# Tile addresses at multiples of 512 bytes, and a final norm split between two engines, in a two-layer trunk

## The chip, the cores and the metric

The kernel runs on one core of one Trainium2 chip. The metric is the time of one execution on the device, in microseconds. The engines are named as in the profile: PE (TensorE's matmuls), PEld (its weight loads), DVE (VectorE), ACT (ScalarE), POOL (GpSimd) and SP (SyncE, which here only issues transfers).

## The reference

A float32 trunk of two layers on 512 tokens of 1024 channels. Layer 0 mixes with a gated linear recurrence (LRU), layer 1 with a sparse attention of three branches; each is followed by a gated FFN with a short convolution, and the whole ends with one more norm:

```python
for layer in range(DEPTH):
    h = h + mixer(rmsnorm(h, mixer_norm_g), ...)          # LRU in layer 0, attention in layer 1
    h = h + conv_ffn(rmsnorm(h, ffn_norm_g[layer]), ...)  # (gelu(conv(a)) * b) @ w_out, 3072 wide
return rmsnorm(h, final_norm_g)
```

```python
def rmsnorm(x, g):
    y = x * lax.rsqrt(jnp.mean(x * x, axis=-1, keepdims=True) + EPS)
    return y * g
```

## The kernel before

Channels lie on the 128 partitions, tokens along the columns, so the activation `x` is 8 tiles of 128 x 512 float32. Every large product is made of three matmuls of 512 columns (`mm3`, lines 211 to 218): weights and activations are each split into a high and a low part in a reduced float32 format, and high x high, high x low and low x high are summed in PSUM. The activation is the moving operand; the weights, 128 x 128 at a time, are the stationary one. ScalarE makes the high part of a weights tile of 128 x 1024, DVE the low part (`_split`, line 178), some tiles ahead of their use. A weights tile serves 8 such slices, 24 matmuls. `wtile` (line 151) puts two of three weights tiles (`whi`, `wlo`) into the pool `wp`, each third one (`whix`, `wlox`) into the pool `wx`; in the FFN's output two tiles of the first kind, 48 matmuls, and one of the second, 24, follow each other.

Order of the work: LRU input (to 130.76 us of the profiled execution), LRU output (to 188.20), FFN input (to 452.10), FFN output (to 585.44), the attention's projections, its scheduled part (676.10 to 875.55, whose order on all engines is written out by hand with a step for each operation), its output (to 898.12), and the second FFN. The last output tile of the second FFN (`m` = 7) is done in two halves of 256 tokens, so that the final norm of the first half (`final`, line 369) runs under the matmuls of the second. `final` sums the squares by a matmul with a column of ones, takes the power on GpSimd, spreads the result over the partitions with a matmul by the identity (`ident`, in `cst`), and then DVE multiplies 8 tiles in place, each one sent off by a transfer of 128 KB, in turn from SP's and ScalarE's queue.

Where the tiles lie: a pool takes its tiles in the order of their first use, each size rounded up to 32 bytes per partition, and the pools lie one behind the other. In the program before, the constants' pool `cp` starts at byte 16,512 of a partition, which leaves 128 when it is divided by 512. The remainders modulo 512 are:

| tiles | remainder before |
|---|---|
| `cst` | 128 |
| `xh`, `xl` (moving, all input products) | 320 |
| `whi`, `wlo` (stationary) | 320 |
| `whix`, `wlox` (stationary) | 0 |
| `fh`, `fl` (moving, FFN output) | 0 |
| `hh`, `hl`, `ch`, `cl`, `ghi`, `glo` (LRU) | 160 |
| `K2h`, `K2l`, `V2`, `P` (attention) | 0 |
| `qa`, `qb` | 256 |
| `ph` | 64 |
| `oh`, `ol` | 128, from the second half on 0 |

Slices of a tile begin at multiples of 512 bytes in all the large products, so a remainder holds for the whole tile.

Of the kernel before, what the change touches and what calls it, by code (L numbers as in the profile page):

```python
# [10 lines left out]
F32 = mybir.dt.float32  # L11
F32R = mybir.dt.float32r
AF = mybir.ActivationFunctionType
# [4 lines left out]
NT = 512  # L18
KD = 8
NB = 10  # L20
NF = 24
DMA = 3
SSQ = (1, 1, 1, 1)
# [47 lines left out]
P_LRUG, P_NSAG, P_FFNG, P_FING = 0, 8, 16, 32  # L71
# [3 lines left out]
P_END = 380  # L75

C_ID, C_D, C_DC, C_SC, C_ROW, C_ONE, C_SL = 0, 128, 640, 768, 776, 777, 778
C_END = 794
# [22 lines left out]
class Trunk:  # L101
# [166 lines left out]
    def norm_finish(self, newps):  # L268
        T, V = self.T, self.V
        ps = newps()  # L270
        for t in range(4):
            T.matmul(ps[:, t:t + 1], self.ssum[:, 128 * t:128 * t + 128], self.cst[:, C_ONE:C_ONE + 1],
                     start=True, stop=True)
        v = self.np_.tile([128, 4], F32, name="nv", bufs=1)
        V.tensor_scalar(v, ps[:, :4], 1.0 / 1024.0, 1e-6, op0=ALU.mult, op1=ALU.add)
        self.rtok = self.np_.tile([128, 4], F32, name="rtok", bufs=1)
        self.G.tensor_tensor(self.rtok, v, self.mhalf, op=ALU.pow)
# [9 lines left out]


    def start(self):
# [6 lines left out]
        self.mhalf = self.cp.tile([128, 4], F32, name="mhalf")  # L296
        self.V.memset(self.mhalf, -0.5)
        warm = self.cp.tile([128, 4], F32, name="warm")
        self.S.activation(warm, self.mhalf, AF.Copy)
# [12 lines left out]
        nc.sync.dma_start(self.prm[:, P_CW:], a["prm"][:, P_CW:])  # L312
# [10 lines left out]
    def run(self):  # L323
# [33 lines left out]
        if self.next_split or seq[-1][:3] != "ffn":  # L357
            for _ in self.final(slice(0, NT), self.ring(0, 1)):
                pass
# [9 lines left out]
    def final(self, ts, newps, sq=None):  # L369
# [10 lines left out]
        v = self.np_.tile([128, 4], F32, name="fv")  # L380
        V.tensor_scalar(v[:, :n], ps[:, :n], 1.0 / 1024.0, 1e-6, op0=ALU.mult, op1=ALU.add)
        rt = self.np_.tile([128, 4], F32, name="frt")
# [222 lines left out]
    def softplus(self, hp):  # L605
# [18 lines left out]
        sp = hp.tile([128, 2, NB], F32, name="sp")  # L624
# [5 lines left out]
    def ffn(self, l):  # L630
        S, V, prm = self.S, self.V, self.prm
        col = lambda c: prm[:, c:c + 1]
        with ExitStack() as s:
# [36 lines left out]
            if not self.next_split:  # L670

                m = KD - 1
                ws = [self.w() for c in range(3)]
                fin = iter(())
                for hf in range(2):
# [9 lines left out]
                    fin = self.final(ts, newacc, sq[:, :256])  # L685
# [14 lines left out]
    def nsa(self):  # L700
        S, V, G, T, prm, cst = self.S, self.V, self.G, self.T, self.prm, self.cst
        tc, a = self.tc, self.a
        with ExitStack() as s:
# [9 lines left out]
            gtok = kp.tile([128, 4, 48], F32, name="gtok")  # L713
# [188 lines left out]
            junk = self.np_.tile([128, 4], F32, name="nv", bufs=1)  # L902
# [22 lines left out]
            def compressed(g, s0, d, newps=None):  # L925
# [39 lines left out]
                def norm():  # L965
                    sm = st["sm"] = ap_.tile([128, 4, 4], F32, name="smc", bufs=1)
# [41 lines left out]
            def scores(g, i, brs, steps):  # L1008
# [280 lines left out]
```

## Time and profile before

| | |
|---|---|
| median of 3 runs | 1311.29 us (1311.05 to 1311.66) |
| profiled execution | 1311.32 us |
| its span, first to last instruction | 1309.5 us |
| mean granted clock of TensorE | 0.996 |
| busy: PE, PEld, DVE, ACT, POOL | 1295.0, 1062.5, 787.2, 612.8, 242.2 us |

Matmuls are pipelined: one shows some 390 ns of its own, but the next starts long before it ends. So the distance from start to start is what a stretch of matmuls costs, and it is read from the starts in the timeline or as a stage's length by its count. Starts are shown to 0.01 us.

### The profile page before, as it was taken

Reading aid. Unit: us, or ns where it says so; the run is one execution under the profiler, and the core shown is the slowest. Engines: PE = TensorE matmul, PEld = TensorE weight load, DVE = VectorE, ACT = ScalarE, POOL = GpSimd, SP = SyncE. Lnnn points to the kernel's source line nnn. Section 1 sums busy time; section 2 is a strip of 40 time slices with the busy share of each in tenths; the row PEclk is TensorE's granted clock in tenths of the full one; section 3 lists DMA queues with packets and bytes.
Section 4 is the critical chain, followed back from the end, with each engine's and each line's share of the span. In section 5 each row is a group of like instructions: output and inputs, shape, how many; then the busy total and the mean of one; then the engine's idle time right before and its main releaser. Section 6 shows DMA issues by size and latency. Waiting matters only on the chain.

```text
span 1309.5 us, 16269 instructions
## 1 busy us (share of the span) xinstructions
PE 1295.0 (99%) x6158; PEld 1062.5 (81%) x6158; DVE 787.2 (60%) x1270; ACT 612.8 (47%) x983; POOL 242.2 (18%) x254
## 2 busy tenths in 40 slices
PE   9999999999999999999999999999999999999996
PEld 7888888888888888888787778888888888888886
DVE  7899875555555533327557978875655555542222
ACT  6788743333333322222458878865433333332220
POOL 0222440000000001115017667633000000000110
PEclk9999999999999999999999999999999999999998
DMA  7232232232232222223311010113222232222221
GB/s 243 89 100 85 90 97 97 97 97 97 97 97 97 96 98 97 90 101 121 121 66 33 33 33 33 34 33 129 97 97 97 97 97 97 97 97 96 89 73 65
DMA packets 36222, 117.71 MB, mean 90 GB/s; under 512 B 4144, under 2 KB 7728, under 8 KB 36144
## 3 DMA queue, kind: packets, MB, share of 16 engines
q1 hardware_dynamic: 34848, 115.61, 26.5%
q8 instruction: 48, 0.79, 0.3%
q10 hardware_dynamic: 1296, 1.07, 0.2%
q14 instruction: 30, 0.25, 0.1%
HBM read 114.57 MB, written 2.10 MB: 89 GB/s over the span
## 4 chain that ended last, share of the span: by engine, by line
PE 94%; DVE 2%; ACT 1%; issue 1%; POOL 1%; DMA 0%; SPq 0%; POOLq 0%; DVEq 0%; ACTq 0%
PE bank L213 28%; PE bank L214 28%; PE bank L215 27%; PE bank L1081 2%; PE bank L1101 1%; PE bank L1097 1%; PE bank L873 1%; PE bank L1027 1%; PE bank L1028 1%; PE bank L832 1%; PE bank L831 1%; PE bank L833 1%; DVE P L1040 0%; PE bank L1100 0%; ACT P L228 0%
## 5 line engine op out<-in xcount | busy, mean ns | idle before, releaser
L213 PE MATMUL bank<-xh,whi 128*128 128x512 f32 x760 | 297.8, 392 | 0.5 <-DVE qn L754 0.2
L215 PE MATMUL bank<-xh,wlo 128*128 128x512 f32 x760 | 296.2, 390 | 0.5 <-DVE wlo L185 0.5
L214 PE MATMUL bank<-xl,whi 128*128 128x512 f32 x760 | 296.2, 390 | 0.3 <-DVE xl L256 0.3
L184 ACT ACTIVATE whi<-wraw 128x1024 fp32r<-128x1024 f32 x143 | 151.3, 1058 | 303.8 <-PE bank L214 251.1
L185 DVE TENSOR_TENSOR wlo<-wraw,whi 128x1024 fp32r<-128x1024 f32 x133 | 163.5, 1230 | 127.4 <-ACT whi L184 117.0
L266 POOL TENSOR_TENSOR ssum<-ssum,sq 128x512 f32<-128x512 f32 x27 | 44.8, 1658 | 766.3 <-issue 581.1
L213 PEld LDWEIGHTS bank<-xh,whi 128*128 128x128 f32 x760 | 142.8, 188 | 32.5 <-DVE nm L1040 0.8
L215 PEld LDWEIGHTS bank<-xh,wlo 128*128 128x128 f32 x760 | 142.6, 188 | 31.0 <-DVE wlo L185 1.0
L214 PEld LDWEIGHTS bank<-xl,whi 128*128 128x128 f32 x760 | 142.8, 188 | 29.6 <-DVE xl L256 0.8
L184 ACT ACTIVATE whix<-wrawx 128x1024 fp32r<-128x1024 f32 x57 | 60.4, 1060 | 131.0 <-PE bank L214 129.6
L214 PE MATMUL bank<-xl,whix 128*128 128x512 f32 x296 | 116.5, 394 | 0.0
L213 PE MATMUL bank<-xh,whix 128*128 128x512 f32 x296 | 116.1, 392 | 0.0
L215 PE MATMUL bank<-xh,wlox 128*128 128x512 f32 x296 | 115.1, 389 | 0.0
L213 PE MATMUL bank<-fh,whi 128*128 128x512 f32 (+1 forms) x272 | 104.0, 382 | 0.0
L214 PE MATMUL bank<-fl,whi 128*128 128x512 f32 (+1 forms) x272 | 103.9, 382 | 0.0
L215 PE MATMUL bank<-fh,wlo 128*128 128x512 f32 (+1 forms) x272 | 103.9, 382 | 0.0
L1057 POOL TENSOR_SCALAR P<-P,c,gtok 128x512 f32<-128x512 f32 (+3 forms) x128 | 79.4, 634 | 99.9 <-DVE c L1053 85.2
L185 DVE TENSOR_TENSOR wlox<-wrawx,whix 128x1024 fp32r<-128x1024 f32 x57 | 70.8, 1242 | 40.9 <-ACT whix L184 40.8
L648 DVE TENSOR_TENSOR ar<-bank,rbc 128x512 f32<-128x512 f32 x48 | 33.2, 691 | 99.6 <-PE bank L215 99.6
L658 DVE TENSOR_TENSOR b<-bank,rbc 128x512 f32<-128x512 f32 x48 | 33.2, 691 | 86.2 <-PE bank L215 86.2
L228 ACT ACTIVATE P<-P,nm 128x512 f32<-128x512 f32 (+3 forms) x128 | 70.9, 556 | 16.9 <-DVE nm L1040 13.8
L228 ACT ACTIVATE t<-t 128x512 f32<-128x512 f32 x48 | 30.4, 632 | 98.0 <-DVE t L654 98.0
(219 smaller groups left out, 2311.5 us busy)
## 6 DMA issues: line engine op xcount, KB each, us to landing
wraw<-in_ffn_in_dram SPq DMA_DIRECT2D x65, 512.0 KB, 3.3
wraw<-in_ffn_out_dram SPq DMA_DIRECT2D x32, 512.0 KB, 3.3
wrawx<-in_ffn_in_dram SPq DMA_DIRECT2D x31, 512.0 KB, 3.3
wrawx<-in_ffn_out_dram SPq DMA_DIRECT2D x16, 512.0 KB, 3.2
wraw<-in_nsa_in_dram SPq DMA_DIRECT2D x16, 512.0 KB, 3.3
wraw<-in_lru_in_dram SPq DMA_DIRECT2D x12, 512.0 KB, 3.7
w<-in_cmp_w_dram SPq DMA_DIRECT2D x8, 512.0 KB, 4.5
wraw<-in_nsa_out_dram SPq DMA_DIRECT2D x8, 512.0 KB, 3.3
```

The lines of the kernel that those rows point to most:

```text
L184: self.S.activation(hi[:, c], raw[:, c], AF.Copy)
L185: (eng or (self.G if self.manual and WLO else self.V)).tensor_sub(lo[:, c], raw[:, c], hi[:, c].bitcast(F32))
L213: ins = mm(ps, wh, xh, start=first, stop=False)
L214: mm(ps, wh, xl, start=False, stop=False)
L215: end = mm(ps, wl, xh, start=False, stop=last)
L228: ins = self.S.activation(out, in_, func, **k)
L266: self.sq_eng.tensor_add(self.ssum, self.ssum, sq)
L648: V.tensor_mul(ar, pa, self.rbc)
L658: V.tensor_mul(b, pb, self.rbc)
L831: T.matmul(pv[t], xh[:, ts], hi[:, sl], start=(k == 0), stop=False)
L1057: G.tensor_scalar(Ps[g, i, br][r], Ps[g, i, br][r], st["c"][:, br, r:r + 1], gtok[:, i, gc:gc + 1], op0=ALU.mult, op1=ALU.mult)
L1081: T.transpose(st["t", kt][:, 128 * r:128 * r + 128], Ps[u][r][:, 128 * kt:128 * kt + 128], self.ident)
```

## The change

Small tiles that only DVE, ScalarE or GpSimd use (and `gtok`) move from the pools of the stages into `cp`, ahead of `cst` or between `cst` and `prm`; `prm` grows by 4 columns and `sp` from 20 to 112, so that the tiles that follow begin elsewhere. `mx` and `smc` of the attention become one tile. In the final norm the sums of `ssum` for both token blocks come before those of `sq`; ScalarE copies the spread norm to SBUF; GpSimd makes the products of `x` tiles 4, 5 and 6 from that copy, and since it multiplies two operands only, ScalarE scales these three tiles by the norm's gain beforehand; DVE makes the other five. The products go to new tiles of two, and a transfer takes two of them (256 KB). The diff, cut to its core:

```diff
+FG = (4, 5, 6)
 def start(self):
-        self.prm = self.cp.tile([128, P_END], F32, name="prm")
-        self.cst = self.cp.tile([128, C_END], F32, name="cst")
+        one = lambda name, shape: self.cp.tile([128] + shape, F32, name=name)
+        few = lambda name, shape, n: [one(f"{name}{j}", shape) for j in range(n)]
+        self.few = {"sm": few("sm", [2, 4], 3), "nm": few("nm", [2, 4], 2), "c": few("c", [2, 4], 3),
+                    "mx": few("mx", [16], 1)}
+        fv, self.mhalf = one("fv", [4]), one("mhalf", [4])
+        self.cst = one("cst", [C_END])
+        self.gtok = one("gtok", [4, 48])
+        self.nv, self.rtok = one("nv", [4]), one("rtok", [4])
+        self.few["fv"], self.few["frt"] = [self.nv, fv], few("frt", [4], 2)
+        self.prm = one("prm", [P_END + 4])
 def softplus(self, hp):
-        sp = hp.tile([128, 2, NB], F32, name="sp")
+        sp = hp.tile([128, 112], F32, name="sp")[:, :2 * NB].rearrange("p (a n) -> p a n", a=2)
 def final(self, ts, newps, newout, sq=None):
-        for t in range(n):
-            for j, p in enumerate(parts):
+        for j, p in enumerate(parts):
+            for t in range(n):
                 T.matmul(ps[:, t:t + 1], p[:, 128 * t:128 * t + 128], self.cst[:, C_ONE:C_ONE + 1],
-                         start=(j == 0), stop=(j == len(parts) - 1))
+                         start=(j == 0 and t == 0), stop=(j == len(parts) - 1 and t == n - 1))
...
-        for k in range(KD):
-            x = self.x[k][:, ts]
-            if "raw" not in self.stages:
-                V.scalar_tensor_tensor(x, x, prm[:, P_FING + k:P_FING + k + 1], ps[:, :128 * n],
+        rb = self.np_.tile([128, NT], F32, name="sq")
+        self.S.activation(rb[:, :128 * n], ps[:, :128 * n], AF.Copy)
+        outs = [newout() for _ in range(KD // 2)]
+        for k in (0, 1, 4, 2, 5, 3, 6, 7):
+            x, o = self.x[k][:, ts], outs[k // 2][:, k % 2, :128 * n]
+            if k in FG:
+                self.G.tensor_mul(o, x, rb[:, :128 * n])
+            else:
+                V.scalar_tensor_tensor(o, x, prm[:, P_FING + k:P_FING + k + 1], ps[:, :128 * n],
                                        op0=ALU.mult, op1=ALU.mult)
-            (self.nc.scalar if k % 2 else self.nc.sync).dma_start(self.a["out"][k][:, ts], x)
+        for j, q in ((0, self.nc.sync), (1, self.nc.scalar), (2, self.nc.sync), (3, self.nc.scalar)):
+            q.dma_start(self.a["out"][2 * j:2 * j + 2, :, ts].rearrange("k p t -> p k t"), outs[j][:, :, :128 * n])
 def ffn(self, l):
                 m = KD - 1
+                for k in FG:
+                    S.activation(self.x[k], self.x[k], AF.Copy, scale=prm[:, P_FING + k:P_FING + k + 1])
...
 def nsa(self):
-            gtok = kp.tile([128, 4, 48], F32, name="gtok")
+            gtok = self.gtok
...
-                    st["mx"] = ap_.tile([128, 16], F32, name="mx", bufs=1)
+                    st["mx"] = self.next("mx")
...
-                    sm = st["sm"] = ap_.tile([128, 4, 4], F32, name="smc", bufs=1)
+                    sm = st["sm"] = st["mx"].rearrange("p (i r) -> p i r", i=4)
...
-                        st["sm"] = ap_.tile([128, 2, 4], F32, name="sm", bufs=3)
-                        st["nm"] = ap_.tile([128, 2, 4], F32, name="nm")
-                        st["c"] = ap_.tile([128, 2, 4], F32, name="c", bufs=3)
+                        st["sm"] = self.next("sm")
+                        st["nm"] = self.next("nm")
+                        st["c"] = self.next("c")
```

The new output tiles take turns in the buffers of `ar`, `t` and `b`, which the FFN no longer uses by then.

## Rows read from the trace of the kernel before

**Rows 1.** Page, part 1: busy time, share of the span and instructions by engine.
```profile
PE 1295.0 (99%) x6158; PEld 1062.5 (81%) x6158; DVE 787.2 (60%) x1270; ACT 612.8 (47%) x983; POOL 242.2 (18%) x254
```
**Rows 2.** Page, part 4: the chain that ended last, its shares by engine.
```profile
PE 94%; DVE 2%; ACT 1%; issue 1%; POOL 1%; DMA 0%; SPq 0%; POOLq 0%; DVEq 0%; ACTq 0%
```
**Rows 3.** Waits of PE, largest sum: who for whom, us in all, times, longest.
```profile
PE bank L321 <- DVE mhalf L297: 1.4, 1, 1.4
```
**Rows 4.** Timeline of PE, FFN output: start us, us, engine, line, operation, out<-in.
```profile
502.10 0.40 PE L213 MATMUL bank<-fh,whi 128*128 128x512 f32 x1
...
513.30 0.39 PE L213 MATMUL bank<-fh,whix 128*128 128x512 f32 x1
...
514.69 0.39 PE L213 MATMUL bank<-fh,whix 128*128 128x512 f32 x1
...
518.77 0.40 PE L213 MATMUL bank<-fh,whi 128*128 128x512 f32 x1
```
**Rows 5.** Timeline of PE, FFN input.
```profile
299.25 0.39 PE L213 MATMUL bank<-xh,whix 128*128 128x512 f32 x1
...
304.74 0.39 PE L213 MATMUL bank<-xh,whi 128*128 128x512 f32 x1
...
311.99 0.39 PE L215 MATMUL bank<-xh,wlo 128*128 128x512 f32 x1
```
**Rows 6.** Stretches of PE, one by stage: from:to, us, PE busy (matmuls), clock, DMA, GB/s.
```profile
23.33:130.76 107.43, 107.43 (x480) 1.00 0.31 97
130.76:188.20 57.44, 57.44 (x247) 1.00 0.27 90
200.89:452.10 251.21, 251.21 (x1108) 1.00 0.30 97
452.10:585.44 133.34, 133.34 (x578) 1.00 0.27 91
...
676.10:875.55 199.45, 197.50 (x1195) 1.00 0.10 33
875.55:898.12 22.57, 22.57 (x98) 1.00 0.29 94
```
**Rows 7.** Timeline of all engines, the end; in brackets idle time before and its releaser.
```profile
1294.36 3.22 DVE L392 SCALAR_TENSOR_TENSOR x<-x,prm,bank 128x256 f32<-128x256 f32 x8 [3.25 <-PE bank L387]
...
1296.87 0.28 PE L215 MATMUL bank<-fh,wlo 128*128 128x256 f32 x1
...
1297.50 0.41 DVE L682 TENSOR_TENSOR x<-bank,x 128x256 f32<-128x256 f32 x1
1298.06 0.42 ACT L684 ACTIVATE sq<-x 128x256 f32<-128x256 f32 x1 [9.78 <-DVE x L682]
...
1298.52 0.38 PE L378 MATMUL bank<-cst,sq 128*128 128x1 f32 x2 [1.26 <-ACT sq L684]
...
1298.99 0.36 PE L378 MATMUL bank<-cst,sq 128*128 128x1 f32 x2
...
1301.64 3.22 DVE L392 SCALAR_TENSOR_TENSOR x<-x,prm,bank 128x256 f32<-128x256 f32 x8 [2.09 <-PE bank L387]
```
**Rows 8.** Single lines: duration ns min/median/max, first and last start us.
```profile
L428 DVE SCALAR_TENSOR_TENSOR xc<-xr,prm,xc x30: 736/750/1711, 30.5 to 139.7; 128x511 f32<-128x511 f32 x10, 128x510 f32<-128x510 f32 x10, 128x509 f32<-128x509 f32 x10
...
L1090 DVE TENSOR_TENSOR sq<-bank,ph x80: 664/683/693, 690.5 to 874.4; 128x512 fp32r<-128x512 f32 x80
...
L740 POOL TENSOR_TENSOR qa<-qn,qa x6: 1278/1288/1293, 683.4 to 801.5; 64x512 fp32r<-64x512 f32 x6
...
L963 POOL TENSOR_TENSOR X<-X,cst x16: 397/402/1374, 691.3 to 820.3; 128x128 f32<-128x128 f32 x16
```
**Rows 9.** The output's transfers, line 394: issue to landing.
```profile
DMA to landing us min/median/max: 1.7/1.7/3.2
```
**Rows 10.** DMA from 1290 to 1312 us in 40 slices: GB/s moved.
```profile
GB/s 0 0 0 0 0 0 0 0 0 0 207 302 348 333 339 341 37 0 0 0 0 0 0 125 324 315 367 294 315 142 17 24 0 0 0 15 0 0 0 0
```

More of the change, by code (lines that the diff above doesn't have):

```diff
@@ L273, in norm_finish @@
                      start=True, stop=True)
-        v = self.np_.tile([128, 4], F32, name="nv", bufs=1)
+        v = self.nv
         V.tensor_scalar(v, ps[:, :4], 1.0 / 1024.0, 1e-6, op0=ALU.mult, op1=ALU.add)
-        self.rtok = self.np_.tile([128, 4], F32, name="rtok", bufs=1)
         self.G.tensor_tensor(self.rtok, v, self.mhalf, op=ALU.pow)
@@ L286, in norm_spread, with next @@
         self.S.activation(self.rbc, ps, AF.Copy)
+    def next(self, name):
+        t = self.few[name]
+        t.append(t.pop(0))
+        return t[-1]
     def start(self):
         nc, a = self.nc, self.a
-        self.prm = self.cp.tile([128, P_END], F32, name="prm")
-        self.cst = self.cp.tile([128, C_END], F32, name="cst")
+        one = lambda name, shape: self.cp.tile([128] + shape, F32, name=name)
[8 more added lines that the diff above has]
+        self.prm = one("prm", [P_END + 4])
         self.x = [self.cp.tile([128, NT], F32, name=f"x{k}") for k in range(KD)]
@@ L295, in start @@
         self.tins, self.tgrp, self.manual = [], None, False
-        self.mhalf = self.cp.tile([128, 4], F32, name="mhalf")
         self.V.memset(self.mhalf, -0.5)
-        warm = self.cp.tile([128, 4], F32, name="warm")
-        self.S.activation(warm, self.mhalf, AF.Copy)
+        self.S.activation(self.nv, self.mhalf, AF.Copy)
         self._dma(0)
@@ L311, in start @@
         nc.sync.dma_start(self.cst, a["cst"])
-        nc.sync.dma_start(self.prm[:, P_CW:], a["prm"][:, P_CW:])
+        nc.sync.dma_start(self.prm[:, P_CW:P_END], a["prm"][:, P_CW:])
         self.ident = self.cst[:, C_ID:C_ID + 128]
@@ L357, in run @@
         if self.next_split or seq[-1][:3] != "ffn":
-            for _ in self.final(slice(0, NT), self.ring(0, 1)):
-                pass
+            raise ValueError("the last stage is a feed-forward one")
         wx.close()
@@ L367, in resid, with final @@
             self.norm_add(m, self.next_split)
-    def final(self, ts, newps, sq=None):
+    def final(self, ts, newps, newout, sq=None):
         T, V, prm = self.T, self.V, self.prm
@@ L375, in final @@
         ps = newps()
-        for t in range(n):
-            for j, p in enumerate(parts):
+        for j, p in enumerate(parts):
+            for t in range(n):
                 T.matmul(ps[:, t:t + 1], p[:, 128 * t:128 * t + 128], self.cst[:, C_ONE:C_ONE + 1],
-                         start=(j == 0), stop=(j == len(parts) - 1))
-        v = self.np_.tile([128, 4], F32, name="fv")
+                         start=(j == 0 and t == 0), stop=(j == len(parts) - 1 and t == n - 1))
+        v = self.next("fv")
         V.tensor_scalar(v[:, :n], ps[:, :n], 1.0 / 1024.0, 1e-6, op0=ALU.mult, op1=ALU.add)
-        rt = self.np_.tile([128, 4], F32, name="frt")
+        rt = self.next("frt")
         self.G.tensor_tensor(rt[:, :n], v[:, :n], self.mhalf[:, :n], op=ALU.pow)
@@ L672, in ffn, with newout @@
                 m = KD - 1
+                for k in FG:
+                    S.activation(self.x[k], self.x[k], AF.Copy, scale=prm[:, P_FING + k:P_FING + k + 1])
+                turn = []
+                def newout():
+                    turn.append("abt"[len(turn) % 3].replace("a", "ar"))
+                    return p.tile([128, NT], F32, name=turn[-1]).rearrange("p (k t) -> p k t", k=2)
                 ws = [self.w() for c in range(3)]
@@ L684, in ffn @@
                     S.activation(sq[:, :256], self.x[m][:, ts], AF.Square)
-                    fin = self.final(ts, newacc, sq[:, :256])
+                    fin = self.final(ts, newacc, newout, sq[:, :256])
                 for _ in fin:
@@ L900, in nsa @@
                 V.tensor_sub(Vc[rs, i, :, 64:], pkv[rs], Vc[rs, i, :, :64].bitcast(F32))
-            junk = self.np_.tile([128, 4], F32, name="nv", bufs=1)
+            junk = self.nv
             self.tact(junk, self.mhalf, AF.Exp)
```

## The prediction

> **What bounds the kernel now.** I read the page's busy times first: TensorE is busy 99% of a span of 1309.5 us [rows 1]. Busy alone proves little, so the chain that ended last comes next: 94% of the span lies on PE, and nothing else has more than 2% [rows 2]. Then TensorE's waits: the largest sum behind any one releaser is 1.4 us in the whole run [rows 3]. So TensorE issues one matmul behind another nearly all the time, and the kernel takes as long as the spacing of some 5,000 matmuls of 512 columns says. What the reader should look for next is therefore not an idle engine but the distance from one matmul's start to the next one's.
>
> That distance isn't the same everywhere. In the FFN output the moving tile is `fh`/`fl`, at remainder 0 modulo 512 bytes. Against `whi`/`wlo`, at remainder 320, 48 matmuls take 513.30 - 502.10 = 11.20 us, 233.3 ns each; against `whix`/`wlox`, at remainder 0, the next 24 take 5.47 us, and once six have gone by, the last 18 take 4.08 us, 226.7 ns each [rows 4]. In the FFN input the moving tile `xh`/`xl` is at 320, and it is the other way round: against the weights at 0, 24 matmuls take 304.74 - 299.25 = 5.49 us, 228.8 ns each; against those at 320, 32 take 7.25 us, 226.6 ns each [rows 5]. In the LRU output the moving tiles are at 160, the weights at 320 or 0, and its 246 matmuls of 512 columns take 57.44 us, 233.5 ns each [rows 6]. The same weights tile is thus fast with one moving tile and slow with the other. What the fast pairs share is an equal remainder (0 with 0, 320 with 320). That is the evidence on which the forecast rests.
>
> **The change, part by part.** Addresses first. The pool of constants starts at remainder 128. The small tiles now ahead of `cst` take 384 bytes, each rounded up to 32: eight of 32 (`sm`, `nm`, `c`), one of 64 (`mx`), two of 32 (`fv`, `mhalf`). So `cst` starts at remainder 0. `cst` 3200, `gtok` 768, `nv`, `rtok` and two `frt` 128 and `prm` 1536 make 5632 = 11 x 512, so `x`, `xh`, `xl` and all pools behind them start at 0; `sp` padded to 448 brings the LRU's tiles to 0 too, and with the small tiles gone from the attention's pool its `ph`, `ch`, `oh` are at 0. So each large product has the pair (0, 0), whose settled spacing is 226.7 ns [rows 4].
>
> The gain by stage is the stage's time less its count of 512-column matmuls times 226.7 ns [rows 6]:
> - LRU input, from 23.33 us: 408 + 54 matmuls are 104.7 us, with 1.6 us of small ones 106.3 of 107.43; I take 0.9 of the 1.1.
> - LRU output: 240 + 6 are 55.8 of 57.44: 1.7 us.
> - FFN input: 46 tiles of 24 are 250.3 of 251.21: 0.9 us, and twice that for the two layers: 1.8.
> - FFN output: 576 are 130.6 of 133.34: 2.7 us; the second layer has 7/8 of it in this form: 2.4. Together 5.1.
> - Attention's output: 96 are 21.8 of 22.57, of which I leave 0.1 to waits: 0.7 us.
> - Attention's scheduled part, 199.45 us: about 512 such matmuls (192 projections, 96 outputs, 192 values, 32 scores) next to remainders 64, 128, 256 and 320. No row separates them; the nearest are the 228.8 and 233.5 ns above, so each can give 2 to 7 ns, 1.0 to 3.6 us together. I take 5 ns, 2.5 us. The schedule is written out by hand, and where another engine is late the gain shrinks to nothing: the lower end is 0.
> - Attention's projections: 0.2 us, as in the FFN input's slow third.
> - The 96 matmuls of 256 columns against `whi` in the last tile: nothing, since no row here shows how short ones settle; the same 3% of some 96 x 113 ns bounds it at 0.3 us either way.
>
> These sum to 12.9 us. DVE, ACT and the weight loads hide behind TensorE in all of it, and 1% faster matmuls don't uncover them: DVE is busy 60% of the span [rows 1].
>
> Now the end of the kernel, where TensorE waits for the norm [rows 7]. The last matmul ends at 1296.87 + 0.28 = 1297.15, but the residual add starts at 1297.50, because DVE still has the eight products of the first half before it (1294.36 to 1297.58). With five on DVE these end about 1.2 us sooner, and the add starts at once: 0.3 us. The sums of squares: behind the wait for `sq` stand today three products of two passes each (the first starts at 1298.52, the third runs from 1298.99, 0.47 us later); in the new order the two of `ssum` run ahead of the wait and two stay, so one step of some 0.23 us goes. Then the eight products on DVE, 3.22 us from the spread. New: DVE does five, 2.0 us; GpSimd first waits for ScalarE's copy of the spread, 0.42 us by the square of the same size [rows 7], and does three. A GpSimd product of 512 columns takes 1.29 us, one of 128 takes 0.40 [rows 8]; on the line between them 256 columns take 0.70. So 0.42 + 3 x 0.70 = 2.5 us: 0.7 us sooner; with the ends of the two rows as bounds (0.40 and 1.29 each) it is DVE's 2.0 us, 1.2 sooner, or 4.3 us, 1.1 later.
>
> The same GpSimd products are the place where a rule speaks against the change. DVE operations with two SBUF operands swell next to GpSimd: the taps on `xr` and `xc` take 736 to 1711 ns; those with one PSUM operand don't, the 80 subtractions from a bank take 664 to 693 ns in the part of the attention where GpSimd works beside them [rows 8]. The final product reads `x` and a bank, so it is of the second kind, and I add nothing. The Trainium skill (SBUF — State Buffer, section "SBUF: two separate sides") says that DVE and GpSimd share one port pair as an exclusive lock, which a DVE operation with two SBUF inputs takes; by the lock the two chains would run in series, and the trace agrees that it is the two-SBUF kind that suffers.
>
> In series the products would cost 2.0 + 3 x 0.70 + 0.42 = 4.5 us instead of 3.22, 1.3 us later, which is my upper bound for this part.
>
> The transfers: 4 of 256 KB instead of 8 of 128 KB for each half. The last one lands 3.2 us after its issue, the median is 1.7 [rows 9]. Twice the bytes add 128 KB at the 340 GB/s of the first half's transfers [rows 10], 0.4 us, so 2.1 to 3.6 us; I take 2.1, nearer the row that most have, and gain 1.1 us, with 0.4 us of loss as the other end. The end gives 0.3 + 0.2 + 0.7 + 1.1 = 2.3 us. The three scalings by ScalarE (`x` 4 to 6) run under the last tile's matmuls, at no cost; if that cover were gone they would cost three times something between 0.42 us and twice that, for 512 columns instead of 256.
>
> The profiled execution took 1311.32 us, with 1309.5 us of span and 1.8 around it; it is 0.03 us above the median, so the two are one for this purpose. 1311.3 - 12.9 - 2.3 = **1296.1 us**.
>
> **The rivals.** (1) The phase settles less well: in each chunk the pair (0, 0) begins slower, 24 matmuls at 227.9 ns on average instead of 226.7 [rows 4]. If this comes back at each tile, 4,800 x 1.2 ns = 5.8 us are lost: **1301.9 us**. For it: those six slow steps. Against: they stand behind a stretch with unequal remainders, which will be gone. (2) The spacing hangs on something else than the remainder, or the tiles don't land where I count: only the end changes, **1309.0 us**, which is within 0.2% (2.6 us, about what a measurement can tell). Against: the two FFN stages, where the same weights swap places. The Trainium skill (SBUF — State Buffer, section "SBUF: two separate sides") would stand on this side: it says that TensorE never waits on anyone at SBUF, and lists its weight loads on a read port of their own. The trace disagrees: 233.3 against 226.7 ns with no wait between. (3) Slower: with everything at remainder 0, also the tiles that ScalarE, DVE and the DMAs fill beside the matmuls, the writes fall into step with TensorE's two reads. The place is every FFN stage; the price is the dearest spacing seen, 233.5 ns, instead of today's mean of about 229.5 ns: 4,800 x 4 = 19 us, less 2.3, **1328 us**; it decides from a mean above 230. Against: in the FFN input today, moving, stationary and freshly written weights are all at 320, and that is the 226.6 ns stretch. (4) GpSimd runs in series with DVE at the end and the last transfer lands late: 2.0 and 1.5 us back, 1299.6 us; inside the range.
>
> **How the numbers follow.** Forecast, with (4) in it: 0.77. Rival 1: 0.14. Rival 2: 0.05. Rival 3: 0.04. Low end: 3.6 instead of 2.5 in the attention, all of 1.1 in the LRU input, 0.3 at the short matmuls, and a spacing 0.6 ns lower, which is what starts rounded to 0.01 us leave open over 18 steps (2.9 us): 1296.1 - 4.5 = 1291.6. High end: rival 1 with a third of (4)'s 3.5 us, 1303. Faster 0.91, same 0.05, slower 0.04.
>
> **What would show it.** In the trace after: 226 to 227 ns in all four stretches, the FFN output near 130.6 us, the LRU output near 55.8 us; the attention's part near 197 us. At the end two products behind the wait for `sq`, the add right behind the last matmul, GpSimd's third product some 2.5 us behind the spread, and DVE's five still at 0.39 us steps. The forecast is wrong if a stretch keeps 229 ns or more, or if the first six matmuls of each tile stay slow.

## The result and the profile after

| | before | after | difference |
|---|---|---|---|
| time, median of 6 executions each (range), us | 1311.17 (1310.36 to 1311.66) | 1300.67 (1299.87 to 1301.96) | 10.5 less |
| ratio after to before, 95% interval | | 0.9921 (0.9908 to 0.9934) | |
| the profiled execution, us (its span) | 1311.32 (1309.5) | 1300.34 (1298.2) | 11.0 less (11.3) |
| start of the last matmul of the FFN, us | 1296.87 | 1287.09 | 9.8 less |

The change is faster by 0.8%. The forecast was 1296.1 us with a range from 1291.6 to 1303: sign and range held, and the gain was 4.7 us smaller than the 15.2 us foretold. The stretches of TensorE, one for each stage, show where it came from and where it did not (from:to in us, length, PE busy and its matmuls, granted clock, DMA share, GB/s). The first six answer to [rows 6]:

```profile
22.89:129.53 106.64, 106.64 (x479) 1.00 0.31 97
129.53:185.73 56.20, 56.20 (x248) 1.00 0.28 91
198.64:449.00 250.36, 250.36 (x1108) 1.00 0.29 97
449.00:579.56 130.56, 130.56 (x578) 1.00 0.28 93
670.27:869.32 199.05, 197.14 (x1195) 1.00 0.10 33
869.32:891.38 22.06, 22.06 (x98) 1.00 0.30 96
891.38:1154.38 263.00, 263.00 (x1170) 1.00 0.30 100
1154.38:1268.73 114.35, 114.35 (x506) 1.00 0.27 88
```

The last two stages, the second layer's FFN, looked like this in the kernel before:

```profile
898.12:1161.94 263.82, 263.82 (x1170) 1.00 0.30 100
1161.94:1278.70 116.76, 116.76 (x506) 1.00 0.26 86
```

But for the norm's sums and spread in the last tile, both kernels issue the same matmuls in the same order, so one stretch stands against the other, from the same matmul to the same matmul:

| stage | before, us | after, us | gained | foretold |
|---|---|---|---|---|
| LRU input | 107.43 | 106.64 | 0.79 | 0.9 |
| LRU output | 57.44 | 56.20 | 1.24 | 1.7 |
| FFN input, both layers | 251.21 + 263.82 | 250.36 + 263.00 | 1.67 | 1.8 |
| FFN output, both layers | 133.34 + 116.76 | 130.56 + 114.35 | 5.19 | 5.1 |
| attention's scheduled part | 199.45 | 199.05 | 0.40 | 2.5 |
| attention's output | 22.57 | 22.06 | 0.51 | 0.7 |
| everything else up to the last matmul | | | 0.0 | 0.2 |
| sum | | | 9.8 | 12.9 |

"Everything else" is 0.4 us gained in the first 23 us (the start differs by as much between executions), and 0.2 us lost each ahead of the first FFN and in the short matmuls of the last tile; the attention's projections, for which 0.2 us were foretold, gained nothing (90.66 and 90.71 us). In the FFN output the spacing is now the same for all three weight tiles and from the first matmul of a tile on (timeline of PE, the first matmul of each group of 24 in that stage's third tile, and the first of the next tile, answering [rows 4]):

```profile
481.64 0.39 PE L214 MATMUL bank<-fh,whi 128*128 128x512 f32 x1
...
487.08 0.39 PE L214 MATMUL bank<-fh,whi 128*128 128x512 f32 x1
...
492.52 0.39 PE L214 MATMUL bank<-fh,whix 128*128 128x512 f32 x1
...
497.96 0.39 PE L214 MATMUL bank<-fh,whi 128*128 128x512 f32 x1
```

Each 24 take 5.44 us, 226.7 ns a matmul; before, the same three groups took 5.60, 5.59 and 5.47 us.

The end of the kernel answers to [rows 7] (start us, us, engine, line, operation; in brackets the idle time before and who ended it):

```profile
1287.09 0.28 PE L216 MATMUL bank<-fh,wlo 128*128 128x256 f32 x1
...
1287.41 0.42 DVE L709 TENSOR_TENSOR x<-bank,x 128x256 f32<-128x256 f32 x1 [0.34 <-PE bank L216]
...
1288.40 0.61 PE L391 MATMUL bank<-cst,sq 128*128 128x1 f32 x4 [0.68 <-ACT sq L711]
1290.03 0.71 PE L400 MATMUL bank<-cst,frt 128*128 128x128 f32 x4 [1.02 <-POOL frt L396]
...
1290.83 0.38 ACT L403 ACTIVATE sq<-bank 128x256 f32<-128x256 f32 x1 [2.49 <-PE bank L400]
1291.25 0.87 DVE L410 SCALAR_TENSOR_TENSOR b<-x,prm,bank 128x256 f32<-128x256 f32 x2 [2.05 <-ACT sq L403]
1291.30 1.41 POOL L408 TENSOR_TENSOR ar<-x,sq 128x256 f32<-128x256 f32 x2 [1.32 <-ACT sq L403]
...
1292.67 0.72 POOL L408 TENSOR_TENSOR b<-x,sq 128x256 f32<-128x256 f32 x1
...
1293.42 0.45 ACTq L413 DMA_DIRECT2D out_dram<-b  x1
```

The add starts 0.32 us behind the last matmul (0.63 before), the products are done at 1293.4, which is 6.3 us behind the last matmul (8.0 before, with a spread of 1.22 instead of 0.71 us in it). But the output's transfers land later than the 1.7 us that most needed before [rows 9]:

```profile
DMA to landing us min/median/max: 2.2/3.0/3.7
```

### The profile page after: what moved, and what is told of

Read it like the earlier page. It is cut to its first block, busy times and chain, and to the rows that moved or that the text cites. A ratio compares the mean times of both kernels' runs of the same rounds, so it can differ in the third digit from the quotient of the medians.

```text
span 1298.2 us, 16261 instructions
## 1 busy us (share of the span) xinstructions
PE 1284.8 (99%) x6158; PEld 1062.2 (82%) x6158; DVE 785.1 (60%) x1264; ACT 615.4 (47%) x988; POOL 245.6 (19%) x260
## 4 chain that ended last, share of the span: by engine, by line
PE 94%; DVE 2%; ACT 1%; POOL 1%; DMA 1%; issue 1%; SPq 0%; POOLq 0%; ACTq 0%; DVEq 0%
PE bank L214 28%; PE bank L215 28%; PE bank L216 28%; PE bank L1108 2%; PE bank L1128 1%; PE bank L1124 1%; PE bank L900 1%; PE bank L1054 1%; PE bank L1055 1%; PE bank L860 1%; PE bank L858 1%; PE bank L859 1%; DVE P L1067 0%; PE bank L1127 0%; ACT P L229 0%
```

## Experiments

All runs, with the medians and the ratio to the kernel before on the same chip. "Data" is the time from the start of the last matmul to the last byte of output in the profiled execution, "spread" how long the four passes of the spread took there (0.71 us where the granted clock is 1.00, that is 2.4 GHz, 1.22 where it has fallen to 0.50, 1.2 GHz, ahead of them; between the two where it fell during them). A "data" is to be compared with one that has a like "spread".

| kernel | median (range), executions | ratio, 95% interval | data, us | spread, us |
|---|---|---|---|---|
| before | 1311.17 (1310.36 to 1311.66), 6 | | 10.8 | 1.22 |
| changed | 1300.67 (1299.87 to 1301.96), 6 | 0.9921 (0.9908 to 0.9934) | 9.5 | 0.71 |
| changed, again | 1300.69 (1300.38 to 1301.26), 4 | 0.9919 (0.9906 to 0.9933) | 9.9 | 1.09 |
| addresses only | 1299.88 (1299.32 to 1300.91), 5 | 0.9919 (0.9905 to 0.9932) | 8.9 | 0.75 |
| addresses only, again | 1299.69 (1299.51 to 1300.91), 4 | 0.9913 (0.9900 to 0.9927) | 9.3 | 1.14 |
| final norm only | 1310.71 (1309.53 to 1312.23), 11 | 0.9999 (0.9990 to 1.0008) | 10.3 | 1.22 |
| all remainders 160 | 1302.80 (1301.28 to 1304.57), 4 | 0.9941 (0.9925 to 0.9958) | 10.7 | 1.22 |
| all remainders 160, again | 1302.15 (1301.13 to 1303.04), 5 | 0.9931 (0.9918 to 0.9945) | 10.1 | 0.71 |
| `fh`, `fl` shifted | 1305.19, 1 | | 10.6 | 1.22 |
| interrupted | 1327.19, 1 | | 9.5 | 0.71 |
| first pair first | 1299.96 (1299.72 to 1300.67), 4 | 0.9918 (0.9905 to 0.9932) | 9.3 | 1.11 |
| single transfers | 1301.04 (1300.59 to 1302.61), 5 | 0.9928 (0.9915 to 0.9940) | 9.2 | 0.71 |
| late load | 1299.70 (1299.54 to 1301.29), 4 | 0.9916 (0.9901 to 0.9931) | 8.9 | 0.71 |
| two banks | 1300.06 (1299.69 to 1300.34), 4 | 0.9914 (0.9900 to 0.9927) | 9.1 | 0.71 |

### The two halves of the change apart

The old final norm on the new addresses, against the changed kernel:

```
-        for j, p in enumerate(parts):
-            for t in range(n):
+        for t in range(n):
+            for j, p in enumerate(parts):
...
+        for k in range(KD):
+            x = self.x[k][:, ts]
+            if "raw" not in self.stages:
+                V.scalar_tensor_tensor(x, x, prm[:, P_FING + k:P_FING + k + 1], ps[:, :128 * n],
...
+            (self.nc.scalar if k % 2 else self.nc.sync).dma_start(self.a["out"][k][:, ts], x)
```

> The changed kernel's addresses with the old final norm (old order of the sums, eight products on DVE, eight transfers of 128 KB for each half). Theory A, the addresses carry the gain that is seen up to the last matmul (9.8 us in the two traces): 1311.2 - 9.8 = 1301.4 us, the last matmul at about 1287, the FFN output at 226.6 ns a matmul, and the end as before (about 1.2 us between the last matmul's start and the first sum of `sq`, the last products 3.2 us). Theory B, the final norm carries more than the trace of one run shows, and the addresses less (for example 7 us): about 1304 us. If the addresses did nothing: 1311 us.

And the other half, the old list of tiles in `start` and in the attention, with the new `final` and what the FFN hands to it:

```
-        self.cst = one("cst", [C_END])
...
-        self.prm = one("prm", [P_END + 4])
+        self.prm = self.cp.tile([128, P_END], F32, name="prm")
+        self.cst = self.cp.tile([128, C_END], F32, name="cst")
...
-        sp = hp.tile([128, 112], F32, name="sp")[:, :2 * NB].rearrange("p (a n) -> p a n", a=2)
+        sp = hp.tile([128, 2, NB], F32, name="sp")
```

> The old addresses with the new final norm. Theory A: the time up to the last matmul stays (233 ns in the FFN output against whi), and the end gives what the traces show, 1.5 us (products done 1.1 us sooner, the spread 0.5 us shorter because it runs at a granted clock of 1.00, the last transfer some 0.6 us later after its issue): 1309.7 us. Theory B, the prediction's sum for the end: 2.3 us, 1308.9 us. Theory C, the transfers of 256 KB give back all that the products gain: 1311 us.

Measured: 1299.88 us with the addresses alone, 1310.71 us with the new final norm alone, against 1311.27 for the kernel before on that chip. **The addresses carry the whole gain; the new end gives nothing that can be measured.** The FFN output's mean spacing is 226.7 ns with the addresses alone and 231.5 ns with the new final norm alone, as in the kernel before. The addresses alone came out below the 1301.4 us of their theory A, and the new final norm at the 1311 of its theory C. Then both ends on the new addresses once more, side by side on one chip:

> The changed kernel once more, so that it stands on one chip beside the kernel with the old final norm, the one with all remainders at 160 and the one with a second spread. Its first runs had a median of 1300.67 us. Theory A: the same, 1300.3 to 1301.0 us; executions fall into two groups about 1.2 us apart, by whether TensorE waits for the compression weights.

> The new addresses with the old final norm, once more, beside the changed kernel on one chip: the difference is the new final norm alone. Theory A, from the two traces: the new one has its products done 1.1 us sooner and loses 1.7 us in the transfers; the old one ends 0.6 us sooner: 1299.9 us, 0.3 to 1.0 us below the changed kernel. Theory B, the prediction's: the new final norm gains 2.3 us, so this kernel is 2.3 us above the changed one.

1299.69 against 1300.69 us: 1.0 us in favour of the old end, after 0.8 us in the first runs, which did not stand side by side. The changed kernel's four executions (1300.38 to 1301.26) did not fall into the two groups expected. The ranges overlap, so the runs alone don't prove a loss, but the order is the same both times, and the traces agree: at a like spread the last byte comes 0.6 us later with the new end both times (9.5 against 8.9 us, 9.9 against 9.3). In the kernel with the old end (first run) the eight products and their transfers read:

```profile
1287.16 0.28 PE L216 MATMUL bank<-fh,wlo 128*128 128x256 f32 x1
...
1290.62 0.75 PE L400 MATMUL bank<-cst,frt 128*128 128x128 f32 x4 [1.02 <-POOL frt L396]
1291.41 3.22 DVE L405 SCALAR_TENSOR_TENSOR x<-x,prm,bank 128x256 f32<-128x256 f32 x8 [1.62 <-PE bank L400]
```

and its output's transfers from issue to landing:

```profile
DMA to landing us min/median/max: 1.7/1.7/1.8
```

The products are done 7.5 us behind the last matmul, 1.2 later than in the changed kernel; but each 128 KB leaves as its product is done, the last one lands 1.8 us after its issue, and the last byte is out 8.9 us behind the last matmul, 0.6 sooner than the 9.5 of the changed kernel at the same clock. The 3.2 us that the prediction took for the old last landing [rows 9] have a cause that shows: in the profiled execution of the kernel before, an instruction fetch of 8 KB on one DMA engine, at 1304.70 us and 1.4 us long, stood in the way of that engine's share of the last transfers. Fifteen engines were done at 1306.26, the sixteenth at 1307.62. How often that happens to this kernel isn't known, since only one of its executions has a trace. The DMA view of the kernel before, 1304.4 to 1307.7 us, shows the fetch as a queue of its own and the one engine at work to the end at some 25 GB/s:

```profile
GB/s 397 311 286 447 360 372 211 224 335 372 372 249 298 372 372 298 174 286 372 360 323 124 25 25 12 25 25 25 25 25 0 0 25 25 25 25 25 25 12 0
q14 instruction: 1, 0.01, 2.6%
```

### Is it the multiple of 512, or that both are equal?

```
-        self.prm = one("prm", [P_END + 4])
+        self.prm = one("prm", [P_END + 4 + 40])
```

> The changed kernel with 40 floats more in `prm`: every tile that TensorE reads, moving or stationary, lies at remainder 160 modulo 512 bytes instead of 0, all equal. Theory A (the prediction's): only the difference between the remainders of the two tiles of a matmul counts. Then nothing changes: 226 to 227 ns settled in every stage, 1300.7 us. Theory B: the multiple of 512 bytes itself counts (a tile at 160 is slower with any partner). Then the FFN output goes to 230 ns or more, and the time to 1305 us or above. In the kernel before, the pair (160, 160) stood only in the LRU's gates, 231.9 ns in chunks that are interrupted, which doesn't decide.

```profile
448.82:579.38 130.56, 130.56 (x578) 1.00 0.28 93
```

The FFN output takes 130.56 us, the same as at remainder 0, and the last matmul starts at 1287.02 us against 1287.09: for TensorE **only the difference of the two remainders counts**. But the time was 1302.80 us. It was run again:

> All remainders at 160, once more: in its first trace the last matmul started at 1287.02 us against 1287.09 at remainder 0, so the spacing is the same, but the median of four executions was 1302.8 us, 2.1 us above the changed kernel's, which the trace doesn't show. Theory A: that was chance (a late weights' load, a late landing): now within 0.8 us of the changed kernel on this chip. Theory B: a remainder of 160 costs time outside the matmuls, for example in transfers: again 1.5 to 2.5 us above it.

1302.15 us, 1.5 above the changed kernel on that chip: the loss is there again, and it is not in the spacing. Part of it is in the transfers of the output, whose tiles now lie at 160 too. From issue to landing, the changed kernel had 2.2/3.0/3.7 us in both its traces, as shown above, and this one (its second) has:

```profile
DMA to landing us min/median/max: 2.3/3.1/4.5
```

The second half's 1 MB moves in 2.9 us from tiles at 0 (both traces of the changed kernel) and in 3.6 us from tiles at 160 (both traces). The next two runs bear it out: 3.6 us with the moving tiles shifted, whose output tiles lie at 384, and 2.9 us in the interrupted kernel, where they lie at 0. That is 0.7 us of the 1.5. In this profiled execution TensorE also waits 1.0 us for the compression weights (below), but the first trace at 160 lacks that wait and some at 0 have it, so what makes up the rest stays open.

### The spacing by difference

```
+PAD = {(0, 8): 16, (0, 16): 48, (1, 0): 8, (1, 8): 24, (1, 16): 64}
...
             for f in range(NF):
...
+                if (l, f) in PAD:
+                    hp.tile([128, PAD[l, f]], F32, name=f"pad{f}")
```

> The changed kernel with the FFN output's moving tiles `fh`, `fl` moved in groups of eight, the weights all at remainder 0: in the first layer 0, 64 and 256 bytes, in the second 32, 128 and 384. One run thus shows the settled spacing for six differences. Theory A: the spacing depends on the difference of the remainders, 226.6 ns for 0 and more for others: 233.3 ns was seen for 192 (0 against 320) and 228.8 for 320 against 0, so something between 228 and 234 for the five others, and the kernel 2 to 5 us slower than the changed one, 1303 to 1306 us. Theory B: only that both are multiples of 64 counts: 226.6 ns for 64, 128, 256 and 384, more for 32 alone: 1301.5 us.

One tile's three groups of 24 matmuls, first layer (differences 0, 64, 256 bytes), then second (32, 128, 384):

```profile
481.78:487.22 5.44, 5.44 (x25) 1.00 0.31 99
487.22:492.73 5.51, 5.51 (x25) 1.00 0.28 95
492.73:498.22 5.49, 5.49 (x25) 1.00 0.28 96
1188.79:1194.38 5.59, 5.59 (x25) 1.00 0.29 94
1194.38:1199.98 5.60, 5.60 (x25) 1.00 0.30 94
1199.98:1205.58 5.60, 5.60 (x25) 1.00 0.27 97
```

Divided by 24 that is 226.7, 229.6, 228.8, 232.9, 233.3 and 233.3 ns. Over all tiles, and without the first eight of each group, the means are 226.6 (0), 228.9 (64), 227.3 (256), 233.3 (32), 232.9 (128) and 233.0 ns (384), beside 233.5 for 192 and 228.8 for 320 (moving less weights) in the kernel before [rows 4, 5]. At 256 the slow steps are all at the head: from the eleventh step on the mean is 226.6 ns there too. So zero is the only difference that is free at once; 256 costs only a slow start of ten steps, 64 and 320 cost 1%, 32, 128, 192 and 384 cost 3%. The slices of a weights tile lie 512 bytes apart, and nothing changes from one to the next. Theory A holds, also in its time (one execution): the last matmul comes 3.9 us later than in the changed kernel.

### Why the attention's part gained so little

```
-                ps = newacc()
+                ps, scr = newacc(), newacc()
+                step = (8, 2)[l]
...
+                    for j in range(0, 8, step):
+                        part = tuple(t[:, 128 * j:128 * (j + step)] for t in w)
+                        self.proj(ps, part, h, range(8 * c + j, 8 * c + j + step), nk=NF)
+                        self.T.matmul(scr[:, :128], self.ident, self.ident, start=True, stop=True)
```

> The changed kernel with small fp32 matmuls of 128 columns into a spare bank set between the matmuls of the FFN output: one after every 24 in the first layer, one after every 6 in the second (but for its last tile); work added, none left out. Theory A: after each interruption some ten matmuls run at 229 to 236 ns, mean 231, before they settle at 226.6. Then in the first layer the matmuls (the one beside the small one left out) have a mean of about 228.5 ns and end each chunk at 226 to 227; in the second they stay near 231 ns, as in the attention's scheduled part. Theory B: interruptions don't matter, and the attention's 231 ns come from its operands (`cst`, `P`, the keys): 226 to 227 ns in both layers beside the small matmuls.

One chunk of 24 of the first layer: the small matmul, then the first, second, eleventh and last of the chunk; below them the second matmul of a chunk of six of the second layer, and the small one behind that chunk.

```profile
482.61 0.38 PE L692 MATMUL bank<-cst 128*128 128x128 f32 x2
482.74 0.48 PE L214 MATMUL bank<-fh,whi 128*128 128x512 f32 x1
483.06 0.40 PE L215 MATMUL bank<-fl,whi 128*128 128x512 f32 x1
...
485.14 0.39 PE L215 MATMUL bank<-fl,whi 128*128 128x512 f32 x1
...
488.09 0.39 PE L216 MATMUL bank<-fh,wlo 128*128 128x512 f32 x1
...
1199.33 0.39 PE L215 MATMUL bank<-fl,whi 128*128 128x512 f32 x1
...
1200.48 0.38 PE L692 MATMUL bank<-cst 128*128 128x128 f32 x2
```

The chunk of 24 begins at 482.74. From its second matmul to the eleventh there are nine steps in 2.08 us, 231 ns each; from the eleventh to the last, thirteen in 2.95 us, 226.9 ns each. In the chunks of six it is five steps in 1.15 us, 230 ns. Over all chunks of 24 that stand behind a small matmul, step by step from the second matmul on: 235.1, 233.3, 235.7, 224.3, 230.9, 235.8, 228.3, 232.5, 231.0, then 226.4 to 226.9 to the end; the mean is 228.8 ns, as theory A has it. The slow start at a difference of 256 above has the same series (231, 233, 236, 224, 231, 236, 228, 233, 231). **A matmul of another kind unsettles the ones after it for about ten steps, although every remainder is equal.** The attention's scheduled part is made of such chunks. The changed kernel there, a chunk of three and one of fourteen (its second, eleventh and last matmul, between two matmuls of another kind):

```profile
700.18 0.40 PE L214 MATMUL bank<-xh,whi 128*128 128x512 f32 x1
700.41 0.39 PE L215 MATMUL bank<-xl,whi 128*128 128x512 f32 x1
700.64 0.40 PE L216 MATMUL bank<-xh,wlo 128*128 128x512 f32 x1
700.88 0.60 PE L1108 MATMUL bank<-cst,P 128*128 128x128 f32 x4
...
717.20 0.60 PE L1108 MATMUL bank<-cst,P 128*128 128x128 f32 x4
...
717.87 0.40 PE L1055 MATMUL bank<-K2l,qa 128*128 128x512 f32 x1
...
719.96 0.39 PE L1128 MATMUL bank<-sq,V 128*128 128x512 f32 x1
...
720.64 0.39 PE L216 MATMUL bank<-xh,wlo 128*128 128x512 f32 x1
720.87 0.60 PE L1108 MATMUL bank<-cst,P 128*128 128x128 f32 x4
```

The two steps of the first chunk are 0.23 us each. In the second, the nine steps from the second matmul to the eleventh take 2.09 us, 232 ns each, and the last three 0.68 us, 227 ns each: what the interrupted FFN shows, in the attention itself. Its 538 matmuls of 512 columns come in 95 chunks, all but one of them of at most fifteen, and only 27 steps lie behind the eleventh matmul of their chunk. These gained: 229.9 ns on average before, 227.0 now. The steps between the second and the eleventh, leaving out those with a wait, had 231.4 ns before and have 230.6 now. So most of this part never settles, at any remainder.

### Other ends

Four variants of the end asked whether the new products can be made to pay. The first two change the transfers alone:

```
+            if j > 1:
+                self.tc.add_manual_dep(sent[j], sent[j - 2].name, ...)
```

> The changed kernel, but each queue issues its first pair of tiles before its second: SyncE (0,1) then (4,5), ScalarE (2,3) then (6,7). Theory A: in the changed kernel the finished pair (0,1) stands behind the issue for (4,5), which waits for GpSimd; 1 MB then moves in one piece and the last landing takes 3.7 us. With the first pair first, 256 KB begin to move about 0.6 us sooner, and the last landing falls to about 3.1 us: 0.6 us faster than the changed kernel, about 1300.1 us. Theory B: the last landing is set by the second pairs alone, which are issued no sooner: no change, 1300.7 us.

```
-        for j, q in ((0, self.nc.sync), (1, self.nc.scalar), (2, self.nc.sync), (3, self.nc.scalar)):
-            q.dma_start(...)
+        for k in (0, 1, 2, 4, 3, 5, 7, 6):
+            e = (self.nc.sync, self.nc.scalar)[k in (1, 4, 5, 6)]
+            ins = e.dma_start(self.a["out"][k][:, ts], outs[k // 2][:, k % 2, :128 * n])
...
```

> The changed kernel, but with eight transfers of 128 KB for each half, four in each queue, each issued as its product is done. Theory A: data begin to move when the first product is done, about 0.8 us sooner than now, and the last transfer has 128 KB less before it: last landing 2.2 us or less behind its issue, which by the four issues of 0.33 to 0.47 us in each queue comes at about the same time as now: 0.8 to 1.4 us faster than the changed kernel, 1299.3 to 1299.9 us. Theory B: four issues in a row in a queue put the last one 0.5 to 0.8 us later, and the gain is 0.3 us or nothing: 1300.4 to 1300.7 us.

With the first pair first the landings fall to at most 3.1 us, as expected, and the data are done 9.3 us behind the last matmul, against 9.9 in the changed kernel's second trace, whose spread took as long. The median is 0.7 us lower, 1299.96, though the runs did not stand side by side and the two intervals overlap. Single transfers gave nothing (1301.04 us): in the profiled execution one DMA engine again carried an instruction fetch (1296.08 us, 0.6 us long) and ended at 1298.91, 0.7 us after the others. That execution, and the one of the final norm alone, also showed a wait of TensorE that the other traces so far lack, with the old addresses and with the new ones (later also the second ones of the addresses only and of all remainders at 160):

```profile
PE bank L907 <- DMA w<-in_cmp_w_dram: 1.1, 1, 1.1
```

It is the last of four reloads of compression weights, between which SyncE had one load for the attention (512 KB). This load was moved behind the reloads, on top of the first pair first:

```
+            if self.w1_name:
+                self.tc.add_manual_dep(ins, self.w1_name, ...)
```

> The kernel with the first pair first, and one load of attention weights (512 KB) on SyncE moved behind the four reloads of the compression weights, whose last one TensorE waited 1.1 to 1.2 us for in some executions (it did in those of the runs with the final norm alone and with single transfers, and did not in the others). Theory A: that load comes 1.4 us sooner, the wait goes from all executions: median 0.5 to 1.2 us below the kernel with the first pair first, 1298.8 to 1299.5 us, and less spread between executions. Theory B: the wait comes from the memory or the queue as such and stays, or the postponed weights are now late in the attention's part: no gain, 1300 us or above.

1299.70 us. In this execution TensorE waited 0.3 us for them, and the reloads moved at some 270 GB/s instead of 370 in the changed kernel's trace. As the trace with the first pair first had no such wait at all, this doesn't show that the order of the loads matters; a gain over 1299.96 can't be told from none. Last, on top of this, two spreads:

```
-FG = (4, 5, 6)
+FG = (6, 7)
...
+        p2 = newps() if ts.start else ps
+        for t in range(n if ts.start else 0):
+            T.matmul(p2[:, 128 * t:128 * t + 128], rt[:, t:t + 1].to_broadcast([128, 128]), ...)
...
-        self.S.activation(rb[:, :128 * n], ps[:, :128 * n], AF.Copy)
+        self.S.activation(rb[:, :128 * n], p2[:, :128 * n], AF.Copy)
...
```

> Another end on the new addresses, with the late load of the kernel before it: for the second half the spread of the norm goes into two banks, one for DVE and one for ScalarE's copy, so that DVE no longer waits 0.45 us for the copy; DVE makes six products and GpSimd two; eight transfers of 128 KB in the order in which the products are done. Theory A: the first product is done 0.45 us sooner, the last at the time it was, and the last data move 0.7 us sooner than with the pairs in order: 1299.0 us, about 0.7 us below that kernel (1299.7). Theory B: 1 MB moves at some 375 GB/s from the first product on and eight issues hold the queues: no gain, 1299.7 to 1300.5 us.

```profile
1290.64 0.71 PE L405 MATMUL bank<-cst,frt 128*128 128x128 f32 x4 [1.03 <-POOL frt L401]
1291.39 0.87 DVE L419 SCALAR_TENSOR_TENSOR b<-x,prm,bank 128x256 f32<-128x256 f32 x2 [1.58 <-PE bank L405]
...
1293.57 1.00 ACTq L424 DMA_DIRECT2D out_dram<-ar  x1
```

DVE now starts 0.04 us behind the spread instead of 0.51, but the last issue comes at 1294.66, no sooner: one of ScalarE's four issues took 1.0 us, and the time is 1300.06 us. Here, too, an instruction fetch (1293.61 us, 0.8 us long) met the transfers, beside the long issue, and one DMA engine ended 0.4 us after the others. Theory B. No variant is measurably faster than the addresses alone.

## Why the prediction was right, and where it was not

**What bounds the kernel, and the pair of remainders: right.** The reading of [rows 4, 5], equal remainders are fast, was the gain. The five rows of the table above whose matmuls come in long runs gave 9.4 us against 10.2 foretold, the FFN output to 0.1 us. The rival by which the address does nothing fell. The Trainium skill (SBUF — State Buffer, section "SBUF: two separate sides"), which stood on its side, says that TensorE never waits on anyone; the traces show no wait on another engine in the FFN's stretches either, but a spacing of 226.6 to 233.5 ns by nothing but where TensorE's own two tiles lie, which the sentence doesn't cover. What in the chip makes the difference is not shown. The slower rival (everything in step at remainder 0) fell as well: no mean above 227 ns in the FFN.

**LRU output, 1.7 foretold, 1.24 measured.** The spacing is as told (median 227 ns). The miss of 0.4 us is four matmuls at 143 to 144 us with gaps of 0.27 to 0.34 us, two of them ahead of matmuls on `hl`, which wait for DVE (timeline of PE's loads and DVE, the second of the two waits):

```profile
143.55 0.69 DVE L521 TENSOR_TENSOR hl<-u,hh 128x512 fp32r<-128x512 f32 x1 [0.15 <-ACT hh L520]
...
144.30 0.18 PEld L215 LDWEIGHTS bank<-hl,whix 128*128 128x128 f32 x1 [0.31 <-DVE hl L521]
```

Before, no gap there was over 0.24 us. The sentence that failed is that DVE and ACT "hide behind TensorE in all of it": here they had no slack of 1%. The same four gaps stand in the runs with all remainders at 160 and with the moving tiles shifted.

**Attention's scheduled part, 2.5 us foretold, 0.40 measured: the wrong step.** The sum gave each of some 512 matmuls 5 ns, the difference between two settled rates. But these matmuls are hardly ever settled: the first ten or so steps of a chunk run at about 231 ns whatever the remainders, as the interrupted FFN shows, and few chunks are longer. The lower bound of 0 stood for another reason (a late engine), and none was late: TensorE's waits in this part are the same in both kernels, 0.4 us the longest. The sign of it was in the trace of before: six slow matmuls at the head of a weights tile in [rows 4] were put down to the unequal stretch ahead of them. That was right for the FFN, where nothing at the head is slow any more, but it wasn't asked what else unsettles a stretch; in the attention nearly all is head. The time came out between rival 4 (1299.6) and rival 1 (1301.9), and neither is its cause as told: rival 1 had the slow heads in the FFN, and of rival 4 only the late last transfer came true.

**The end, 2.3 us foretold, none measured.** Three terms were right in the trace: the add 0.31 us sooner (0.3), the sums 0.2 (from 0.87 to 0.64 us between the first sum of `sq` and `fv`), GpSimd's three products 0.72 us each (0.70), with DVE's steps at 0.39 us beside them, so neither swelling nor the series of rival 4. Two things were not foreseen: DVE's products wait for ScalarE's copy (they start 0.51 us behind the spread instead of 0.04, hidden as long as GpSimd's chain ends last), and of the 1.1 us from the spread's start to the last product (4.48 before, 3.36 after) 0.5 are the spread, which happened to run at the higher clock. The term that failed is the last landing: 2.1 us instead of 3.2 was foretold, a gain of 1.1. The 3.2 came of the instruction fetch in the profiled execution, as the 1.7 and 1.8 of the old end on the new addresses show; and the new one is 3.7. The sum took a landing for a matter of one transfer and its own bytes. But the old end issues 128 KB every 0.39 us, as fast as they move, while the four pairs are issued within 0.7 us and their 1 MB takes 2.9 us, so the last pair lands behind all the others. From 1.8 to 3.7 us this is a loss of 1.9, against which the products' 1.2 us don't suffice. The bound that the prediction gave for it, 0.4 us of loss, was worked out from the same 3.2.

In sum: 12.9 foretold for the addresses, 9.8 in the traces up to the last matmul; 2.3 for the end, between no difference (old addresses) and a loss of 0.8 to 1.0 us (new addresses) by the medians. Those two don't agree fully, and the addresses alone gained 11.0 to 11.4 us by the medians, more than the 9.8. In the traces the last byte then comes 1.9 us sooner behind the last matmul (8.9 against 10.8), of which 0.5 us are the spread's clock and 1.4 us the fetch. So the kernel before may lose some 1 us at its end more often than the others do. That is not shown, as only one of its executions has a trace. That the time fell inside the range is in part luck: the two terms that failed, 2.1 us in the attention and the whole 2.3 us of the end, lie on the same side, and the range reached so far up only for rivals that did not happen as told.

## What to carry to other kernels

Where TensorE is the bound, look at the distance between matmuls by pair of tiles, and lay moving and stationary tiles at equal remainders modulo 512 bytes; the gain is the number of matmuls in long runs times the difference, and chunks of under ten between matmuls of other shapes give next to nothing. A common remainder of 0 did better here than one of 160, because of the output's transfers. A maximum in one trace (a landing of 3.2 beside a median of 1.7) is no term of a sum until what made it is known. Work that is split to make the last product earlier pays only if its bytes also leave earlier, and a landing is priced with all that is queued ahead of it.

## What the runs showed of the hardware

- The spacing of fp32r matmuls of 512 columns depends on the difference of the two operands' start addresses: 226.6 ns at 0, the same at 256 after ten slower steps, 228.9 at 64, 228.8 at 320, 233 at 32, 128, 192 and 384 bytes (modulo 512). A common shift of both by 160 leaves the 226.6.
- After a matmul of another kind, about ten steps are uneven (224 to 236 ns, mean 232) before the rhythm of 226.6 is back.
- The moment at which the granted clock falls at the end differs between executions of one kernel: the changed one's spread took 0.71 us in one trace and 1.09 in the other, with the same wait of 1.02 to 1.03 us ahead of it. In the first the granted clock was 1.00 all through the spread, in the second it fell to 0.50 within it (mean 0.58).
- DVE waits for ScalarE when both read one bank: it starts 0.51 us behind the spread, and 0.04 us with two banks. The Trainium skill (PSUM — Partial Sum Buffer, section "PSUM bank collisions raise a hardware error") tells that two engines must not touch one bank at once, reads too, and that software puts a dependency between them; the trace agrees, DVE's products name ScalarE's copy as what they waited for.
- The four 256 KB transfers of the last half took 2.9 us from tiles at remainder 0 (the changed kernel's two traces, the final norm only, the interrupted kernel) and 3.6 us from tiles at 160 (two traces) and at 384 (the shifted one).
- An instruction fetch of 8 KB that met the last transfers took 1.4, 0.6 and 0.8 us of one DMA engine in three traces, and that engine ended 1.4, 0.7 and 0.4 us after the others.
